# Instance norm on one core: 4 MB units in 32 KB rows against 8 MB units in 64 KB rows, with 4 MB units at both ends

## The chip, the cores and the metric

One core of one Trainium2 chip. The metric is the device time of one execution of the kernel in microseconds, the median of several runs. The core has engines with queues of their own: TensorE (PE) for matmuls, VectorE (DVE), ScalarE (ACT), GpSimd (POOL) and SyncE (SP), which here only issues transfers. Sixteen DMA engines move data between the chip's memory (HBM) and the core's own memory (SBUF, 128 partitions). SP, ACT and POOL each have a DMA queue.

## The reference

For each of 4 x 128 channels (four batches of 8 groups of 16 channels) of 256 x 256 numbers in float32, the mean and the variance over the 65,536 numbers are taken, and the channel is normalised and multiplied by its gamma:

```python
mu = x.mean(axis=(3, 4), keepdims=True)
var = ((x - mu) ** 2).mean(axis=(3, 4), keepdims=True)
x_norm = (x - mu) / np.sqrt(var + 1e-5)
out = x_norm * gamma[None, :, :, None, None]
```

The input is 134.2 MB and so is the output. Each number is read once and written once.

## The kernel before

The 512 channels are taken in 32 units of 16 channels. A channel lies over 8 partitions, so that a unit is a tile of 128 partitions x 8,192 numbers: a row of 32 KB in each partition, 4 MB in all, which is one contiguous stretch of HBM. Six slots of this size (`xt`, line 45) hold the units in SBUF; unit u uses slot u modulo 6.

The order of work on each engine is the order in which the program is written (manual schedule). First come two small transfers on POOL's queue: zeros into a small part of the output (`touch`, line 54, 16 rows of 512 B; the unit's own store writes over them later) and gamma (line 55, 16 rows of 32 B). Then the loads of units 0 to 5 are issued, 1 and 3 on ACT's queue and the others on SP's (lines 56 and 57). VectorE has 60 empty instructions. The averaging matrix `navg` (lines 66 to 76, -1/65,536 within the 8 x 8 blocks of one channel) is made on POOL; gamma is spread over the partitions by a copy on VectorE and eight small matmuls (lines 83 to 94) into `g_col`.

Then for each unit, in the loop from line 105:

- VectorE sums each row (line 107) while ScalarE sums its squares (line 108) into `st`.
- TensorE multiplies `st` by `navg` (line 116), which gives each partition its channel's -mean and -mean of squares (`ps`).
- VectorE makes minus the variance from it (line 117), ScalarE the root (line 121), VectorE the reciprocal (line 125), and the product with gamma (line 127).
- VectorE normalises the tile in place (line 130): (x - mean) * scale.
- ACT issues the store (line 134), and SP the load of unit u + 6 (line 136, line 48), which waits until the store of unit u has landed, for they share the slot.

So in steady work SP's queue holds loads and ACT's queue holds stores, and each of the sixteen DMA engines takes packets from both.

Of the kernel before, what the change touches and what calls it, by code (L numbers as in the profile page):

```python
# [1 line left out]

# [4 lines left out]

F32 = mybir.dt.float32
U8 = mybir.dt.uint8
ALU = mybir.AluOpType  # L10
ACTF = mybir.ActivationFunctionType
AX = mybir.AxisListType


@with_exitstack
def kernel(
    ctx: ExitStack,
    tc: tile.TileContext,
    x: bass.AP,
    gamma: bass.AP,  # L20
    out: bass.AP,
):
    nc = tc.nc
    B, G, C, H, W = x.shape
    P = nc.NUM_PARTITIONS
    HW = H * W
    n_ch = B * G * C
    S = 8
    K = P // S
    F = HW // S  # L30
    U = n_ch // K
    NG = (G * C) // K
    AHEAD = 6
    assert HW % S == 0 and (G * C) % K == 0

    xv = x.rearrange("b g c h w -> (b g c h w)").rearrange("(u p f) -> u p f", p=P, f=F)
    ov = out.rearrange("b g c h w -> (b g c h w)").rearrange("(u p f) -> u p f", p=P, f=F)
    gv = gamma.rearrange("g c -> (g c)")

    data = ctx.enter_context(tc.tile_pool(name="data", bufs=1))  # L40
    singles = ctx.enter_context(tc.tile_pool(name="singles", bufs=1))
    psum = ctx.enter_context(tc.tile_pool(name="psum", bufs=4, space=bass.MemoryType.PSUM))
    ctx.enter_context(tc.manual_schedule())

    slots = [data.tile([P, F], F32, name=f"xt{i}") for i in range(AHEAD)]

    def load(u, queue):
        queue.dma_start(out=slots[u % AHEAD][:], in_=xv[u])  # L48


    g_row = singles.tile([1, G * C], F32, name="g_row")
    touch = singles.tile([16, 128], F32, name="touch")
    nc.vector.memset(touch[:], 0.0)  # L53
    nc.gpsimd.dma_start(out=ov[0][0::S, 0:128], in_=touch[:])  # L54
    nc.gpsimd.dma_start(out=g_row[:], in_=gv[None, :])  # L55
    for u in range(AHEAD):
        load(u, nc.scalar if u in (1, 3) else nc.sync)

    for _ in range(60):
        nc.vector.nop()  # L60

    eps_t = singles.tile([P, 1], F32, name="eps_t")
    nc.gpsimd.memset(eps_t[:], 1e-5)
    one = singles.tile([1, 1], F32, name="one")
    nc.gpsimd.memset(one[:], 1.0)
    navg = singles.tile([P, K, S], F32, name="navg")
    nc.gpsimd.memset(navg[:], -1.0 / HW)  # L67
    nc.gpsimd.affine_select(  # L68
        out=navg[:], in_=navg[:], pattern=[[-S, K], [0, S]], compare_op=ALU.is_ge,
        fill=0.0, base=0, channel_multiplier=1,  # L70
    )
    nc.gpsimd.affine_select(  # L72
        out=navg[:], in_=navg[:], pattern=[[S, K], [0, S]], compare_op=ALU.is_ge,
        fill=0.0, base=S - 1, channel_multiplier=-1,
    )
    navg_w = navg[:].rearrange("p k s -> p (k s)")
    root_eps = singles.tile([P, 1], F32, name="root_eps")
    nc.scalar.activation(out=root_eps[:], in_=eps_t[:], func=ACTF.Sqrt)  # L78
    g_rep = singles.tile([1, NG, K, S], F32, name="g_rep")
    g_ps = psum.tile([P, NG], F32, name="g_ps", bufs=1)  # L80
    g_col = singles.tile([P, NG], F32, name="g_col")

    nc.vector.tensor_copy(  # L83
        out=g_rep[:],
        in_=g_row[:].rearrange("o (n k) -> o n k", n=NG).unsqueeze(3).to_broadcast([1, NG, K, S]),
    )
    for n in range(NG):
        nc.tensor.matmul(  # L88
            out=g_ps[:, n : n + 1],
            lhsT=g_rep[:, n].rearrange("o k s -> o (k s)"),  # L90
            rhs=one[:],
            start=True, stop=True,
        )
    nc.vector.tensor_copy(out=g_col[:], in_=g_ps[:])  # L94

    junk = singles.tile([P, F], U8, name="junk")

    st = singles.tile([P, U, 2], F32, name="st")
    nvar = singles.tile([P, U], F32, name="nvar")
    std = singles.tile([P, U], F32, name="std")  # L100
    rstd = singles.tile([P, U], F32, name="rstd")
    scale = singles.tile([P, U], F32, name="scale")

    squares = []
    for u in range(U):
        t = slots[u % AHEAD]
        nc.vector.reduce_sum(out=st[:, u, 0:1], in_=t[:], axis=AX.X)  # L107
        square = nc.scalar.activation(  # L108
            out=junk[:], in_=t[:], func=ACTF.Square, accum_out=st[:, u, 1:2],
        )  # L110
        if u:

            tc.declare_no_dep(square.ins, squares[-1].ins, reason="junk, ordered by the root between")
        squares.append(square)
        ps = psum.tile([P, 2], F32, name="ps")
        nc.tensor.matmul(out=ps[:], lhsT=navg_w, rhs=st[:, u], start=True, stop=True)  # L116
        nc.vector.tensor_scalar(  # L117
            out=nvar[:, u : u + 1], in0=ps[:, 0:1], scalar1=ps[:, 0:1],
            scalar2=ps[:, 1:2], op0=ALU.mult, op1=ALU.add,
        )  # L120
        nc.scalar.activation(  # L121
            out=std[:, u : u + 1], in_=nvar[:, u : u + 1], func=ACTF.Sqrt,
            bias=eps_t[:], scale=-1.0,
        )
        nc.vector.reciprocal(out=rstd[:, u : u + 1], in_=std[:, u : u + 1])  # L125
        g = u % NG
        nc.vector.tensor_mul(  # L127
            out=scale[:, u : u + 1], in0=rstd[:, u : u + 1], in1=g_col[:, g : g + 1],
        )
        nc.vector.tensor_scalar(  # L130
            out=t[:], in0=t[:], scalar1=ps[:, 0:1], scalar2=scale[:, u : u + 1],
            op0=ALU.add, op1=ALU.mult,
        )
        nc.scalar.dma_start(out=ov[u], in_=t[:])
        if u + AHEAD < U:
            load(u + AHEAD, nc.sync)


# [1 line left out]
_INS = ['x', 'gamma']  # L140
_OUTS = [((4, 8, 16, 256, 256), 'float32')]


# [23 lines left out]
```

## Time and profile before

| what | value |
|---|---|
| time, median of 3 runs (lowest to highest) | 626.78 us (626.75 to 626.82) |
| span of the profiled execution | 625.8 us |
| DMA traffic | 268.46 MB in 9,282 packets, 429 GB/s over the span |
| VectorE busy | 443.4 us (71%) |
| ScalarE busy | 238.8 us (38%) |
| TensorE busy | 21.4 us (3%) |
| row sums (line 107), one | 8,684 ns |
| row sums of squares (line 108), one | 7,030 ns |
| normalising (line 130), one | 4,550 ns |
| median time from issue to landing, loads on SP's queue | 38.5 us |
| the same, stores on ACT's queue | 62.5 us |

The span is the time from the first to the last instruction of one execution that was profiled; the runs are timed without a profile, and include 1.0 us more. An engine's busy share is an average over the whole span. The time from issue to landing of a transfer includes its wait behind earlier transfers of its queue.

### The profile page before, as it was taken

The numbers are of one execution on the slowest core, as the hardware profiler recorded it, in microseconds if no ns is written. First come the engines' busy times: TensorE is split into PE (matmuls) and PEld (weight loads), VectorE is DVE, ScalarE is ACT, GpSimd is POOL, SyncE is SP. The second block draws the span as 40 slices with busy tenths as digits, with TensorE's granted clock in tenths as the row PEclk, the third lists the DMA queues.
The fourth block names the chain that finished last, engine by engine and source line by source line (L and its number), as shares of the span: only waits on it lengthen the run. The fifth ranks groups of instructions, "written<-read, shape, count | busy, mean of one in ns | idle before, by whom it ended". The sixth has DMA issues, their size and how long they took to land.

```text
span 625.8 us, 631 instructions
## 1 busy us (share of the span) xinstructions
PE 21.4 (3%) x80; PEld 19.5 (3%) x80; DVE 443.4 (71%) x163; ACT 238.8 (38%) x98; POOL 2.4 (0%) x11
## 2 busy tenths in 40 slices
PE   0200000000000000000000000000000000000000
PEld 0200000000000000000000000000000000000000
DVE  0588999999776687766776667867668676686730
ACT  0444444444443244432344423444224442244400
POOL 1000000000000000000000000000000000000000
DMA  8999999999999999999999999999999999999998
GB/s 369 436 415 429 429 436 436 436 436 434 424 434 434 434 436 434 431 429 434 436 436 436 436 431 427 431 436 431 436 434 434 429 434 436 436 436 436 429 425 354
DMA packets 9282, 268.46 MB, mean 429 GB/s; under 512 B 1072, under 2 KB 1088, under 8 KB 1088
## 3 DMA queue, kind: packets, MB, share of 16 engines
q10 hardware_dynamic: 4896, 142.61, 52.9%
q1 hardware_dynamic: 4320, 125.83, 46.7%
q0 software_dynamic: 64, 0.01, 0.0%
q14 instruction: 2, 0.02, 0.0%
HBM read 134.22 MB, written 134.23 MB: 429 GB/s over the span
## 4 chain that ended last, share of the span: by engine, by line
another core or an unknown queue 61%; DMA 17%; DVE 15%; SPq 1%; PE 1%; issue 0%; ACT 0%
DVE st L107 10%; DMA xt<-in_x_dram 10%; DMA out_dram<-xt 8%; DVE xt L130 5%; SPq L48 1%; PE ps L116 1%; ACT std L121 0%; DVE nvar L117 0%; DVE rstd L125 0%; DVE scale L127 0%
## 5 line engine op out<-in xcount | busy, mean ns | idle before, releaser
L107 DVE TENSOR_REDUCE st<-xt 128x1 f32<-128x8192 f32 x32 | 277.9, 8684 | 101.2 <-DMA xt<-in_x_dram 101.2
L108 ACT ACTIVATE junk<-xt 128x8192 uint8<-128x8192 f32 x32 | 225.0, 7030 | 276.0 <-DMA xt<-in_x_dram 232.8
L130 DVE TENSOR_SCALAR xt<-xt,ps,scale 128x8192 f32<-128x8192 f32 x32 | 145.6, 4550 | 1.2
L121 ACT ACTIVATE std<-nvar,eps_t 128x1 f32<-128x1 f32 x32 | 9.4, 294 | 79.6 <-DVE nvar L117 79.6
L116 PE MATMUL ps<-st,navg 128*128 128x2 f32 x64 | 17.9, 349 | 558.0 <-DVE st L107 558.0
L116 PEld LDWEIGHTS ps<-st,navg 128*128 128x128 f32 x64 | 16.0, 311 | 559.8 <-issue 559.8
L117 DVE TENSOR_SCALAR nvar<-ps 128x1 f32<-128x1 f32 x32 | 9.2, 287 | 23.8 <-PE ps L116 23.8
L125 DVE RECIPROCAL rstd<-std 128x1 f32<-128x1 f32 x32 | 5.2, 164 | 11.6 <-ACT std L121 11.6
L83 DVE COPY g_rep<-g_row 1x1024 f32<-1x1024 f32 x1 | 0.7, 680 | 14.3 <-DMA g_row<-in_gamma_dram 14.3
L108 ACT ACTIVATION_READ_ACCUMULATOR junk<-xt 128x1 f32 x32 | 6.0, 187 | 0.0
L127 DVE TENSOR_TENSOR scale<-rstd,g_col 128x1 f32<-128x1 f32 x32 | 5.1, 159 | 1.1
L88 PE MATMUL g_ps<-one,g_rep 1*128 1x1 f32 x16 | 3.5, 346 | 16.2 <-DVE g_rep L83 16.2
L88 PEld LDWEIGHTS g_ps<-one,g_rep 1*128 1x128 f32 x16 | 3.5, 325 | 16.1 <-issue 16.1
L94 DVE COPY g_col<-g_ps 128x8 f32<-128x8 f32 x1 | 0.2, 166 | 3.7 <-PE g_ps L88 3.7
L78 ACT ACT_TABLE_LOAD x1 | 1.3, 1283 | 1.7 <-PEq L151 1.7
L53 DVE MEMSET touch<- 16x128 f32 x1 | 0.2, 165 | 0.9 <-PEq L151 0.9
L54 POOL DMA_DIRECT2D out_dram<-touch x1 | 0.6, 619 | 0.8 <-DVE touch L53 0.8
L55 POOL DMA_DIRECT2D g_row<-in_gamma_dram x1 | 0.5, 487 | 0.0
L68 POOL TENSOR_SCALAR_AFFINE_SELECT navg<-navg 128x128 f32<-128x128 f32 x1 | 0.4, 400 | 0.1
L72 POOL TENSOR_SCALAR_AFFINE_SELECT navg<-navg 128x128 f32<-128x128 f32 x1 | 0.4, 399 | 0.1
L67 POOL MEMSET navg<- 128x128 f32 x1 | 0.2, 232 | 0.0
L78 ACT ACTIVATE root_eps<-eps_t 128x1 f32<-128x1 f32 x1 | 0.2, 202 | 0.0
(6 smaller groups left out, 0.6 us busy)
## 6 DMA issues: line engine op xcount, KB each, us to landing
out_dram<-xt ACTq DMA_DIRECT2D x32, 4096.0 KB, 62.5
xt<-in_x_dram SPq DMA_DIRECT2D x30, 4096.0 KB, 38.5
xt<-in_x_dram ACTq DMA_DIRECT2D x2, 4096.0 KB, 31.6
out_dram<-touch POOLq DMA_DIRECT2D x1, 8.0 KB, 9.1
g_row<-in_gamma_dram POOLq DMA_DIRECT2D x1, 0.5 KB, 13.3
```

The lines of the kernel that those rows point to most:

```text
L48: queue.dma_start(out=slots[u % AHEAD][:], in_=xv[u])
L78: nc.scalar.activation(out=root_eps[:], in_=eps_t[:], func=ACTF.Sqrt)
L83: nc.vector.tensor_copy(out=g_rep[:], in_=g_row[:].rearrange("o (n k) -> o n k", n=NG).unsqueeze(3).to_broadcast([1, NG, K, S]),)
L88: nc.tensor.matmul(out=g_ps[:, n : n + 1], lhsT=g_rep[:, n].rearrange("o k s -> o (k s)"), rhs=one[:], start=True, stop=True,)
L107: nc.vector.reduce_sum(out=st[:, u, 0:1], in_=t[:], axis=AX.X)
L108: square = nc.scalar.activation(out=junk[:], in_=t[:], func=ACTF.Square, accum_out=st[:, u, 1:2],)
L116: nc.tensor.matmul(out=ps[:], lhsT=navg_w, rhs=st[:, u], start=True, stop=True)
L117: nc.vector.tensor_scalar(out=nvar[:, u : u + 1], in0=ps[:, 0:1], scalar1=ps[:, 0:1], scalar2=ps[:, 1:2], op0=ALU.mult, op1=ALU.add,)
L121: nc.scalar.activation(out=std[:, u : u + 1], in_=nvar[:, u : u + 1], func=ACTF.Sqrt, bias=eps_t[:], scale=-1.0,)
L125: nc.vector.reciprocal(out=rstd[:, u : u + 1], in_=std[:, u : u + 1])
L127: nc.vector.tensor_mul(out=scale[:, u : u + 1], in0=rstd[:, u : u + 1], in1=g_col[:, g : g + 1],)
L130: nc.vector.tensor_scalar(out=t[:], in0=t[:], scalar1=ps[:, 0:1], scalar2=scale[:, u : u + 1], op0=ALU.add, op1=ALU.mult,)
```

## The change

- A big unit has 32 channels over 4 partitions each: 128 rows of 64 KB, 8 MB. There are 14 of them, in three slots of 64 KB per partition, which take the same space as the six of before.
- Before and after them stand two small units each, of 16 channels as before; a pair shares one slot, half of each row for each. So there are 18 units, numbered 0 to 17: 0, 1, 16 and 17 are small.
- All loads are issued on SP's queue. At the start those of units 0 to 3 are issued. Unit 4 is loaded when units 0 and 1 have been stored; then unit u + 3 when unit u has been stored; units 16 and 17 both after the store of unit 13.
- The squares of a big unit are summed in two halves on ScalarE, into two columns of `st`. The matmul has three columns for it, and one more small instruction of VectorE (`rest`) joins the second half to the root, as its bias.
- There are two averaging matrices, for 8 and for 4 partitions per channel. Gamma is loaded as 32 rows of 4 single numbers, after the four loads have been issued, and is spread by three matmuls with 0/1 matrices. `touch`, the 60 empty instructions and the spreading copy are gone.

The core of the diff:

```diff
-    slots = [data.tile([P, F], F32, name=f"xt{i}") for i in range(AHEAD)]
+    slots = [data.tile([P, FB], F32, name=f"xt{i}") for i in range(SLOTS)]
...
+    def small(pair):
+        nonlocal first, turn
+        for h in range(2):
+            units.append((first, 8, slots[turn % SLOTS][:, h * FS : (h + 1) * FS]))
+            first += KS
+        turn += 1
...
+    small(0)
+    while first < n_ch - KB:
+        units.append((first, 4, slots[turn % SLOTS][:]))
+        first += KB
+        turn += 1
+    small(1)
...
-    nc.gpsimd.dma_start(out=ov[0][0::S, 0:128], in_=touch[:])
-    nc.gpsimd.dma_start(out=g_row[:], in_=gv[None, :])
-    for u in range(AHEAD):
-        load(u, nc.scalar if u in (1, 3) else nc.sync)
...
-    for _ in range(60):
-        nc.vector.nop()
...
+    def load(u):
+        nc.sync.dma_start(out=units[u][2], in_=rows(flat_x, u))
...
+    for u in range(4):
+        load(u)
+    with nc.allow_non_contiguous_dma(reason="128 numbers"):
+        nc.gpsimd.dma_start(out=g_kn[:], in_=gamma.rearrange("g c -> (g c)").rearrange("(n k) -> k n", k=KB))
...
+    for i in range(3):
+        nc.tensor.matmul(out=g_ps[:, i], lhsT=pick[i], rhs=g_kn[:], start=True, stop=True)
     nc.vector.tensor_copy(out=g_col[:], in_=g_ps[:])
...
+        c0, s, t = units[u]
+        parts = 8 // s
+        nc.vector.reduce_sum(out=st[:, u, 0:1], in_=t, axis=AX.X)
+        for h in range(parts):
+            square = nc.scalar.activation(
+                out=junk[:], in_=t[:, h * FS : (h + 1) * FS], func=ACTF.Square,
+                accum_out=st[:, u, 1 + h : 2 + h],
+            )
...
+        if parts == 2:
+            bias = rest[:, u : u + 1]
+            nc.vector.tensor_scalar(
+                out=bias, in0=ps[:, 2:3], scalar1=-1.0, scalar2=1e-5, op0=ALU.mult, op1=ALU.add,
+            )
...
-        nc.scalar.dma_start(out=ov[u], in_=t[:])
-        if u + AHEAD < U:
-            load(u + AHEAD, nc.sync)
+        nc.scalar.dma_start(out=rows(flat_o, u), in_=t)
+        if u == 1:
+            load(4)
+        elif 2 <= u and u + 3 < U - 1:
+            load(u + 3)
+            if u + 3 == U - 2:
+                load(U - 1)
```

## The prediction

> **What bounds the kernel now.** I read the page's row of DMA shares first, then the traffic by queue in a steady stretch, then the queue that SyncE waits with, and last the end of the timeline. The page, its 40 slices (busy tenths of VectorE, of the 16 DMA engines, and GB/s):
>
> ```profile
> DVE  0588999999776687766776667867668676686730
> DMA  8999999999999999999999999999999999999998
> GB/s 369 436 415 429 429 436 436 436 436 434 424 434 434 434 436 434 431 429 434 436 436 436 436 431 427 431 436 431 436 434 434 429 434 436 436 436 436 429 425 354
> ```
>
> The DMA engines are full from the second slice to the last but one, whatever VectorE does (it is at 6 to 7 tenths in the second half). The same by stretches (length, busy engines, then clock, DMA share, GB/s at the end of each line):
>
> ```profile
> 0.00:2.00 2.00, 0.00 (x0) 0.00 (x0) 0.17 (x1) 0.28 (x1) 0.84 (x6) 1.00 0.42 115
> 200.00:500.00 300.00, 8.92 (x32) 8.01 (x32) 216.19 (x80) 117.65 (x48) 0.00 (x0) 1.00 1.00 433
> 586.00:601.00 15.00, 0.56 (x2) 0.50 (x2) 13.71 (x5) 7.42 (x3) 0.00 (x0) 1.00 1.00 430
> 601.00:615.00 14.00, 0.00 (x0) 0.00 (x0) 0.14 (x1) 0.00 (x0) 0.00 (x0) 1.00 1.00 433
> 623.00:626.00 3.00, 0.00 (x0) 0.00 (x0) 0.00 (x0) 0.00 (x0) 0.00 (x0) 1.00 0.03 11
> ```
>
> 433 GB/s in the middle, and the same 430 to 433 at the end, where only stores are left. So direction and mixture cost nothing; only the start (2 us) and the last 2.7 us are not full. In the steady stretch the two queues have equal shares, and each load takes 38.5 us to land, twice its 19.36 us period:
>
> ```profile
> q10 hardware_dynamic: 2224, 65.01, 50.2%
> q1 hardware_dynamic: 2218, 64.82, 50.0%
> ...
> xt<-in_x_dram SPq DMA_DIRECT2D x15, 4096.0 KB, 38.5
> ```
>
> That is because load u+6 is issued when store u has landed, while the load before it is still running:
>
> ```profile
> SPq L48 <- DMA out_dram<-xt: 535.3, 26, 59.6
> ```
>
> And the end: the last load lands at 586.12, its unit is computed in 15.05 us, and its store is issued at 601.17. DMA does not notice, since three stores are queued at 586 (7 equal 4 MB transfers of 9.68 us make up the last 67 us):
>
> ```profile
> 586.12 8.69 DVE L107 TENSOR_REDUCE st<-xt 128x1 f32<-128x8192 f32 x1 [4.33 <-DMA xt<-in_x_dram]
> ...
> 596.59 4.55 DVE L130 TENSOR_SCALAR xt<-xt,ps,scale 128x8192 f32<-128x8192 f32 x1
> 601.17 0.34 ACTq L134 DMA_DIRECT2D out_dram<-xt  x1
> ```
>
> So the time is the bytes at full rate plus idle DMA, and a change can only move the cost of a byte or leave DMA idle. The profiled execution spans 625.8 us, 1.0 below the median of 626.78; I add differences to 626.8.
>
> **How a DMA engine shares.** The trace's packet records: every row of a tile is one packet, 32,768 B in 1,213 ns, and each DMA ends with a 4 B completion packet on each engine. At 7.2 us the GpSimd queue joins the two load queues: on each engine its 512 B row, its completion, the 32 B gamma row and its completion start 2.43 us apart (7.23, 9.67, 12.09, 14.52), which is twice 1,213 ns. So each queue with work gets **one packet a turn, however long it is**. While all rows have 32 KB, that is an equal split. With 64 KB rows beside 32 KB rows it is 2 to 1.
>
> **The change, part by part.**
> 1. *Cost of a byte.* A 512 B packet took 27 ns, a 32 KB one 1,213: 1,186 ns for 32,256 B, 0.03677 ns a byte, and 8 ns fixed. Eight rows of 32 KB are 9.639 us by bytes alone; a DMA takes 19.36/2 = 9.68. So some 0.04 us a DMA are not bytes. 64 DMAs become 36, each still with 8 rows per engine: 28 x 0.042 = **-1.2 us**. No 64 KB row is in this trace. Bounds: 0 (the row is cut into two packets), and -2.7 (64 x 0.042, all of it gone). I take -1.2, the nearest row's law.
>  The Trainium skill (DMA: Bandwidth & Descriptors, Anatomy of one DMA) gives about 2.0 us fixed plus bytes/436 GB/s for one DMA, by which 28 fewer would be worth 56 us. The trace disagrees: 9.68 us from one store's landing to the next, where that law has 11.6. The fixed part lies under the next DMA's data.
> 2. *Start.* All first loads go on SP. Unit 0 is in after about 1.8 + 9.7 + 0.9 = 12.4 us instead of 22.6, but VectorE has g_col's copy ahead of it, which needs gamma. Gamma is now 128 numbers of 4 B, 8 packets and a completion per engine instead of the four turns above; with one load queue a turn is 1.21 us, so 9 x 1.21 = 10.9 from about 7 us, then three of the matmul pairs (3.5/8 = 0.44 each) and the copy: about 20 us, as 19.9 before. DMA has 24 MB of loads (58 us) in hand. Following rows one by one: stores 0 and 1 land at about 64 and 80.5, loads 2 and 3 at 46 and 75, and unit 2 is computed at about 78, so store 2 is there just before store 1 ends. 0, but without slack: each us by which unit 0 starts after 20 leaves up to one us of DMA idle near 80. Bounds 0 and +2. The dropped touch, nops and copies (0.7 us at most each) are beside loads: 0.
> 3. *Middle.* A unit costs VectorE 2 x 8.69 + 1.77 (reduce end to normalise start) + 0.29 (one more L117-like row) + 2 x 4.55 = 28.5 us of a 38.6 us period; the squares, 2 x 7.2, lie beside the reduce. Per slot: load 38.6, compute 28.5, store 38.6, some 3 of landing and issue: 109 against three periods, 116. There is always a store queued; 0. If that fails, stores run alone at the same 433 GB/s, and still nothing is lost.
> 4. *Tail.* Let T be the end of load 15 and store 13. Loads 16 and 17 (32 KB rows) run beside stores 14 and 15 (64 KB rows): a turn of both is 1.21 + 2.41 = 3.62 us. Load 16: 8 turns, T+29.0. Store 15 is there at T + 0.3 (landing) + 28.5 + 0.1 + 1.0 (issue to first packet, 0.81 to 1.80 at the start) = 29.9, so load 17 has one row alone, then 7 turns: T + 55.6. Then 0.3 + 15.05 + 1.0: store 17's first packet at T+72. All other bytes left at T are 7 x 4 MB, done at T + 7 x 9.66 = 67.6. DMA is idle **+4.5 us**, which before's tail was not. Without the row alone it would be 6.9; with an equal split by bytes, 0.
> 5. More waits: SP's load 17 stands right behind load 16, both on store 13; nothing else is queued behind. ACT's next squares stand behind the store's issue, as before. 0.
>
> Sum: 626.8 - 1.2 + 4.5 = **630.1** (profiled span about 629).
>
> **Why T is one point, and the rivals.** After a store lands (0.33 us after its last packet) the next load's packets come 1.0 to 1.6 us later (0.81 to between 1.80 and 2.43 over the engines at the start): 1.35 to 1.95 us, less than one 64 KB row (2.41). So the next store gets one row ahead, then both alternate, and the store's completion waits its turn behind the load's last row: both end in the same round, and this repeats.
> - *Stores lead by a row more* (no loss). If the engines are spread (a store's 16 completions come 0.4 us apart before 150 us, 1.6 after), the wait passes 2.41 us on some and their stores gain a second row. Then at T store 14 has 7 rows left: load 16 takes 7 x 3.62 + 1.21 = 26.6, load 17 is alone until 29.9 (2.7 rows), the other 5.3 turns end at T+49; store 17 starts at T+65.5, DMA has work until 67.6 - 2.4 = 65.2. Idle 0.3: 626.8 - 0.9 = 625.9. It decides from a wait of 2.41 us on. For it: the spread of 1.6; against it: 0.4 in the undisturbed stretch. Chance 0.23, for 625.6 to 628 (partly led).
> - *Late start on top of the tail*: gamma's 4 B packets later than I count. +1 to +3: 631 to 634. Chance 0.15.
> - *Cheaper rows and a covered tail*: -2.7 (part 1's lower end) and 0 to 1 idle, 624.1 to 625.4. Chance 0.12.
> - *The rows are cut in two* (the change does less than it says): two 32 KB packets a row, an even split by bytes, no idle, no gain: 626.5 to 626.8. Its chance is in the first rival's 0.23.
> - *64 KB rows run slower*: the row pitch doubles in HBM; each per cent of a packet's time costs 6.2 us (619.5 us of full DMA), 2 per cent 639. The 1,213 ns show no such loss at 32 KB. Chance 0.05. The Trainium skill (DMA: Bandwidth & Descriptors, Latency and other measured facts) has a rate falling from 214 to 207 GB/s at a 512 KiB row pitch; no run here shows it.
> - The forecast itself, 628 to 632: 0.45.
>
> **How the numbers follow.** About 0.2% (1.25 us) is what a measurement of this kernel can tell from no change. Slower: 0.45 + 0.15 + 0.05 = 0.65. Same: 0.23. Faster: 0.12. The range, 624.5 to 634.0, leaves out the slow rows (0.05) and what of the cheaper rows and of the late start lies farthest out (some 0.1); it takes in parts 1, 2 and 4 up to their ends (0 + 2 + 4.5, or 6.9 alone; -2.3 below).
>
> **What would show it.** In the changed kernel's trace: packets of 65,536 B of about 2,418 ns (1); unit 0's reduce near 20 us, not 12 (2); no DMA slice below 9 tenths between 100 and 600 us (3); load 16 landing about 29 us after load 15 and load 17 26 to 29 us later, and a hole of some 4.5 us in the DMA about 17 us before the end (4). No hole and the loads evenly 19 us apart would make part 4 wrong; a hole near 80 us would make part 2 wrong.

## The result, and the profile after

The changed kernel takes 629.3 us (median of 6 runs, 628.92 to 630.82) beside 626.85 us before (6 runs, 626.75 to 627.51): a ratio of 1.0041, with a 95% interval of 1.003 to 1.0053; the medians lie 2.45 us apart. The forecast was 630.1. Here and below a run that is over 1.5% above the fastest of its kernel counts as slow: it is left out of the ratios (one run each of e5 and e9, two of e12), but not out of the medians. Its profiled execution spans 627.8 us and was timed at 629.47, close to the median; the span of before in the prediction, 625.8, is at the slow end of its own runs (624.9 to 625.9 where it was measured beside the experiments), so that the two profiles differ by 2.0 us and the medians by 2.45.

The page after, the same rows as were shown of before:

```profile
DVE  1978897097692956929569395792948839499780
DMA  9999999999999999999999999999999999999997
GB/s 363 438 401 451 411 457 418 451 418 451 418 447 422 447 422 447 414 451 418 451 418 451 413 455 413 455 405 464 401 468 401 468 401 468 401 447 420 449 411 303
```

DMA is still full. But for the first and the last two slices GB/s swings between 401 and 468 from slice to slice: that is counting, since a packet is counted in the slice where it starts and 64 KB rows are coarse beside 15.7 us slices. By stretches (length, busy engines, clock, DMA share, GB/s):

```profile
400.00:500.00 100.00, 1.68 (x6) 1.50 (x6) 74.51 (x18) 39.44 (x15) 0.00 (x0) 1.00 1.01 438
597.00:612.00 15.00, 0.56 (x2) 0.50 (x2) 13.21 (x5) 7.42 (x3) 0.00 (x0) 1.00 0.95 411
612.00:614.00 2.00, 0.00 (x0) 0.00 (x0) 0.64 (x1) 0.00 (x0) 0.00 (x0) 1.00 0.80 344
620.00:623.00 3.00, 0.00 (x0) 0.00 (x0) 0.00 (x0) 0.00 (x0) 0.00 (x0) 1.00 0.86 371
623.00:628.00 5.00, 0.00 (x0) 0.00 (x0) 0.00 (x0) 0.00 (x0) 0.00 (x0) 1.00 0.17 72
```

The middle is as full as before. The hole that was forecast at the end is there, but shallow: 0.95 and then 0.80 at 597 to 614 us, while the last unit is finished. (A share over two microseconds is coarse, since packets are counted where they start; the packet records below give 0.45 us of idle time for it.) At 620 to 623 us the share is no lower than that of before in the same stretch:

```profile
620.00:623.00 3.00, 0.00 (x0) 0.00 (x0) 0.00 (x0) 0.00 (x0) 0.00 (x0) 1.00 0.83 360
```

But after 623 us 17% of five microseconds is still moved, where before moved 3% of three: the last packet ends later, and the DMA engines do not finish together. The tail's computation, from the timeline:

```profile
578.77 0.34 ACTq L163 DMA_DIRECT2D out_dram<-xt  x1
...
593.70 0.34 ACTq L163 DMA_DIRECT2D out_dram<-xt  x1
597.62 8.69 DVE L128 TENSOR_REDUCE st<-xt 128x1 f32<-128x8192 f32 x1 [3.96 <-DMA xt<-in_x_dram]
...
612.67 0.34 ACTq L163 DMA_DIRECT2D out_dram<-xt  x1
```

These are the stores of units 15, 16 and 17. VectorE waited 3.96 us for load 17, which landed 46.8 us after load 15 (550.84), where two loads at the even pace of before, 19.4 us each, would take 38.8.

**Where the 2 us went.** I added up the packet records of the two traces, as a mean over the 16 engines. Packets at their usual lengths (1,213 ns for 32 KB, **2,418 ns for 64 KB**) come to 621.06 us before and 619.26 after: 1.8 saved. Time by which packets ran longer than that: 1.65 before, 3.04 after, 1.4 lost (0.5 of it in the first 60 us, where before has 1.38 and after 1.89; 0.9 later). Idle engines, from the start to the last packet of any: 3.27 before, 4.92 after, 1.65 lost; of it 0.35 lies near 6 us (six engines wait 0.6 to 1.2 us), 0.45 near 613 us, and the rest, some 0.9, at the end. These three give +1.25 of the +1.78 by which the last packet ends later (626.27 against 624.49); the other 0.5 is the balance of two small items: records of one engine overlap by a few ns, which fewer packets do less (0.8 lost), and there are fewer completions (0.3 saved). The 16 completions of the last store lie 1.6 us apart before and 3.0 after.

### The profile page after: what moved, and what is told of

Read it like the earlier page. It is cut to its first block, busy times and chain, and to the rows that moved or that the text cites. A ratio compares the mean times of both kernels' runs of the same rounds, so it can differ in the third digit from the quotient of the medians.

```text
span 627.8 us, 434 instructions
## 1 busy us (share of the span) xinstructions
PE 11.4 (2%) x42; PEld 10.4 (2%) x42; DVE 429.4 (68%) x105; ACT 234.7 (37%) x84; POOL 6.2 (1%) x21
## 4 chain that ended last, share of the span: by engine, by line
DMA 63%; DVE 26%; another core or an unknown queue 7%; PE 1%; issue 0%; ACT 0%; SPq 0%
DMA xt<-in_x_dram 36%; DMA out_dram<-xt 28%; DVE st L128 16%; DVE xt L159 8%; PE ps L138 1%; ACT std L151 0%; DVE nvar L141 0%; SPq L70 0%; DVE rstd L155 0%; DVE scale L156 0%; DVE rest L148 0%
## 5 line engine op out<-in xcount | busy, mean ns | idle before, releaser
L128 DVE TENSOR_REDUCE st<-xt 128x1 f32<-128x16384 f32 (+1 forms) x18 | 275.8, 15323 | 151.5 <-DMA xt<-in_x_dram 151.5
L159 DVE TENSOR_SCALAR xt<-xt,ps,scale 128x16384 f32<-128x16384 f32 (+1 forms) x18 | 141.7, 7870 | 0.7
L151 ACT ACTIVATE std<-nvar,rest 128x1 f32<-128x1 f32 x14 | 4.1, 294 | 57.0 <-DVE rest L148 57.0
L138 PE MATMUL ps<-st,navg 128*128 128x3 f32 (+1 forms) x36 | 10.0, 349 | 586.4 <-DVE st L128 586.4
L138 PEld LDWEIGHTS ps<-st,navg 128*128 128x128 f32 x36 | 9.0, 311 | 587.4 <-issue 587.4
L141 DVE TENSOR_SCALAR nvar<-ps 128x1 f32<-128x1 f32 x18 | 5.2, 287 | 13.4 <-PE ps L138 13.4
L155 DVE RECIPROCAL rstd<-std 128x1 f32<-128x1 f32 x18 | 3.0, 164 | 6.5 <-ACT std L151 6.5
L151 ACT ACTIVATE std<-nvar,eps_t 128x1 f32<-128x1 f32 x4 | 1.2, 294 | 9.5 <-DVE nvar L141 9.5
L156 DVE TENSOR_TENSOR scale<-rstd,g_col 128x1 f32<-128x1 f32 x18 | 2.9, 159 | 0.6
L148 DVE TENSOR_SCALAR rest<-ps 128x1 f32<-128x1 f32 x14 | 2.1, 148 | 0.0
```

The costliest lines, as they stand in the source:

```text
L128: nc.vector.reduce_sum(out=st[:, u, 0:1], in_=t, axis=AX.X)
L138: nc.tensor.matmul(out=ps[:, : 1 + parts], lhsT=navg[s], rhs=st[:, u, : 1 + parts], start=True, stop=True,)
L141: nc.vector.tensor_scalar(out=nvar[:, u : u + 1], in0=ps[:, 0:1], scalar1=ps[:, 0:1], scalar2=ps[:, 1:2], op0=ALU.mult, op1=ALU.add,)
L148: nc.vector.tensor_scalar(out=bias, in0=ps[:, 2:3], scalar1=-1.0, scalar2=1e-5, op0=ALU.mult, op1=ALU.add,)
L151: nc.scalar.activation(out=std[:, u : u + 1], in_=nvar[:, u : u + 1], func=ACTF.Sqrt, bias=bias, scale=-1.0,)
L156: nc.vector.tensor_mul(out=scale[:, u : u + 1], in0=rstd[:, u : u + 1], in1=gamma_of(u),)
```

## The experiments

Each experiment has one trace, so figures of its DMA engines are of one execution. The theory after reading the two traces was that the loss lies in the tail: 32 KB loads beside 64 KB stores. The rivals were the 64 KB rows themselves, all over the run, and the new start. The median of the kernel before, measured beside each on the same chip, stands in its row.

| run | what it changes in the changed kernel | us (runs) | before, beside it | last store's completions, us apart |
|---|---|---|---|---|
| changed kernel | | 629.30 (6) | 626.85 | 3.0 |
| e1 | stores of units 14 and 15 in 32 KB half rows | 629.13 (5) | 626.88 | 4.1 |
| e2 | all rows 32 KB | 627.84 (11) | 626.88 | 1.0 |
| e3 | gamma on ACT's queue | 632.03 (6) | 626.88 | 0.6, after a hole; 6.6 the store before |
| e4 | no small pair at the end | 642.14 (2) | 626.88 | 0.2, after a hole |
| e5 | e1 and e3 | 630.66 (7) | 627.14 | 4.7 |
| e6 | e2, loads issued later | 628.10 (12) | 627.14 | 1.0 |
| e7 | 64 KB rows, 64 partitions a transfer | 734.74 (4) | 627.14 | |
| e8 | the kernel before, with the new start | 627.65 (11) | 627.14 | 1.6 |
| e9 | only loads in 32 KB half rows | 658.79 (6) | 626.87 | |
| e10 | only stores in 32 KB half rows | 627.64 (11) | 626.87 | 1.2 |
| e11 | the old start | 635.28 (6) | 626.87 | 0.6, after a hole; 5.8 the store before |
| e12 | e2 and the old start | 628.29 (12) | 626.87 | 5.6 |

**e1: the tail's stores in half rows.**

```diff
-        nc.scalar.dma_start(out=rows(flat_o, u), in_=t)
+        if u in (U - 4, U - 3):
+            for h in range(2):
+                nc.scalar.dma_start(
+                    out=rows(flat_o, u)[:, h * FS : (h + 1) * FS], in_=t[:, h * FS : (h + 1) * FS],
+                )
+        else: ...
```

> The changed kernel, but the stores of the last two big units (14 and 15) go as two transfers of 32 KB half rows, so that they share the DMA engines evenly with the loads of units 16 and 17. Theory (the loss is the 2 to 1 turn in the tail, which lets load 17 land 8.8 us later on the engines that are behind, 0.45 us of mean DMA idleness near 612 us and a wider finish): load 17 lands with a spread under 3 us instead of 8.8, no hole at 612 us, about 628.0 us. Rival (64 KB rows cost by themselves, by longer packets all over the run): unchanged at 629.3.

Load 17 landed with a spread of 3.1 us over the engines instead of 8.8, and the hole near 612 us is gone: by the packet records no engine is idle from 600 to 618 us.

```profile
597.00:612.00 15.00, 0.56 (x2) 0.50 (x2) 10.28 (x5) 4.36 (x3) 0.00 (x0) 1.00 1.03 443
612.00:614.00 2.00, 0.00 (x0) 0.00 (x0) 0.00 (x0) 0.00 (x0) 0.00 (x0) 1.00 0.88 377
```

The loss of time stayed: 629.13 (ratio 1.0034, 1.0022 to 1.0046). In this trace the engines were 4.1 us apart in each load from 354 to 513 us, and they finished 4.1 us apart. My theory had taken the tail's hole for the loss; the lag was older than the tail. Up to the store of unit 14 e1 is the same program as the changed kernel, whose engines were 2.6 to 3.1 us apart in that stretch: the lag differs by a microsecond from one execution to another.

**e2: no 64 KB row anywhere.** Each transfer of a big unit is two, and a half load waits for the store of its half only.

```diff
-        nc.sync.dma_start(out=units[u][2], in_=rows(flat_x, u))
+        for h in range(8 // units[u][1]):
+            nc.sync.dma_start(
+                out=units[u][2][:, h * FS : (h + 1) * FS], in_=rows(flat_x, u)[:, h * FS : (h + 1) * FS],
+            )
...
-        nc.scalar.dma_start(out=rows(flat_o, u), in_=t)
+        for h in range(parts):
+            nc.scalar.dma_start(
+                out=rows(flat_o, u)[:, h * FS : (h + 1) * FS], in_=t[:, h * FS : (h + 1) * FS],
+            )
```

> The changed kernel with every big load and store cut into two transfers of 32 KB half rows: same units, slots, order and computation, but no 64 KB packet anywhere. Theory (everything lost comes from the long rows, in the tail and in packets that ran over 2418 ns, and 1.0 us is gained by them): the gain of 1.0 is given back, 1.3 of the tail and up to 1.4 of long packets return, 626.9 to 628. Rival (three slots or the new start cost the time, whatever the rows): 629.3 plus the 1.0 us of fixed packet cost, 630.3.

627.84 us (1.0015, 1.0006 to 1.0023), 1.5 less than the changed kernel though the fixed cost of 28 transfers is back. After 60 us there are all but no long packets (0.1 us in the mean), the engines stay 1.0 us apart to the end, and there is no hole:

```profile
597.00:612.00 15.00, 0.00 (x0) 0.00 (x0) 4.49 (x1) 0.00 (x0) 0.00 (x0) 1.00 1.02 439
620.00:623.00 3.00, 0.00 (x0) 0.00 (x0) 0.00 (x0) 0.00 (x0) 0.00 (x0) 1.00 1.06 459
623.00:626.00 3.00, 0.00 (x0) 0.00 (x0) 0.00 (x0) 0.00 (x0) 0.00 (x0) 1.00 0.04 14
```

So in this kernel the long rows cost more than they save.

**e3 and e5: gamma on ACT's queue.**

```diff
-        nc.gpsimd.dma_start(out=g_kn[:], ...
+        nc.scalar.dma_start(out=g_kn[:], ...
```

> The changed kernel with gamma loaded from ScalarE's queue instead of GpSimd's. In the changed kernel's trace six DMA engines stand idle for 0.6 to 1.2 us near 6.3 us, just before the first packet of GpSimd's queue, and these six are the ones that are late in the tail. Theory (GpSimd's queue causes that hole, and the head start it gives the others is what opens the tail): no hole at 6 us, load 17 lands with a spread under 4 us, about 628.3 us. Rival (the hole comes from the single load queue at the start, or the spread from later long packets): hole and spread stay, 629.3.

> Gamma on ScalarE's queue (as in e3) and the stores of units 14 and 15 in 32 KB half rows (as in e1). e3's trace has a hole of 5.0 us at 613 to 618 us, after load 17 landed 18.6 us later on the last engine than on the first. Theory (the uneven turns in the tail make that hole, from engines that are 7 us apart before it): load 17's spread no wider than before it, no hole, 632.0 - 5.0 = 627 to 629 us. Rival (e3's time comes from gamma's place, not from the tail): 631 to 632.

The hole near 6 us went, the first loads land 0.5 us apart instead of 1.0, and yet e3 takes 632.03 (1.0103, 1.0066 to 1.0139; its runs lie between 631 and 640): the engines drift 7.3 us apart by 506 us all the same, and then the tail has a hole of the size of part 4 of the prediction. Load 17 landed 18.6 us later on the last engine than on the first, and 50.0 us after load 15 on the last engine of each, not 55.6; so the sizes agree, but not the count of rows. The stretches of e3:

```profile
602.00:613.00 11.00, 0.56 (x2) 0.50 (x2) 9.15 (x4) 7.42 (x3) 0.00 (x0) 1.00 0.90 387
613.00:618.00 5.00, 0.00 (x0) 0.00 (x0) 4.70 (x2) 0.00 (x0) 0.00 (x0) 1.00 0.11 46
618.00:628.00 10.00, 0.00 (x0) 0.00 (x0) 0.00 (x0) 0.00 (x0) 0.00 (x0) 1.00 0.98 423
```

For five microseconds VectorE alone works (4.70 of 5.00) and DMA moves a tenth. e5 evens the turns in the tail: no such hole, 630.66 (1.0065, 1.004 to 1.0091), but with its own drift of 4.7 us, and runs from 628.9 up to 643.7. So the tail's uneven turns are real and make a hole of five microseconds where the engines come to it 7 us apart. The drift is another thing: it is there with gamma on either queue.

**e4: the tail's price, exposed.** The loop of big units goes on to the last channel.

```diff
-    while first < n_ch - KB:
+    while first < n_ch:
...
-    small(1)
...
```

> The changed kernel without the small pair at the end: units 0 and 1 small, then 15 big ones to the end. Theory (the price of the tail is compute of the last unit plus issue minus the stores still queued): the last load ends with 6 rows of the store before it left, 14.5 us; 0.3 + 28.4 us of work and 1.0 to the first packet make 29.7; idle 15.2, about 642 us. Rival (the end is hidden or depends on something else): under 635.

642.14 us (1.0241, 1.0224 to 1.0259), as worked out. The last store but one ends at 603.4 to 607.6 us, and the last comes at 619.9:

```profile
603.00:605.00 2.00, 0.00 (x0) 0.00 (x0) 2.00 (x1) 2.00 (x1) 0.00 (x0) 1.00 0.08 33
605.00:619.00 14.00, 0.56 (x2) 0.50 (x2) 12.82 (x6) 0.69 (x3) 0.00 (x0) 1.00 0.01 5
619.00:639.00 20.00, 0.00 (x0) 0.00 (x0) 0.01 (x1) 0.00 (x0) 0.00 (x0) 1.00 0.97 419
```

(Packets count where they start, so the share falls one row early.) The rule, work of the last unit less the stores still queued, holds to a microsecond here: the engines are idle for 15.5 us in the mean between 600 and 620 us, and 15.2 were worked out.

**e6 and e7: is it the load queue that runs nearly dry?** In e6 the two half loads of a unit are issued in the other order, so that both wait for the whole slot; in e7 a transfer takes the even or the odd partitions, with rows left at 64 KB.

e6 beside e2:

```diff
-        for h in range(8 // units[u][1]):
+        for h in reversed(range(8 // units[u][1])):
```

e7 beside the changed kernel (n and parts are 2 for a big unit; stores likewise):

```diff
-        nc.sync.dma_start(out=units[u][2], in_=rows(flat_x, u))
+        for h in range(n):
+            nc.sync.dma_start(out=units[u][2][h::n], in_=rows(flat_x, u)[h::n])
```

> e2 (32 KB half rows everywhere), but the two loads of a unit are issued in the other order, so that both wait for the second store of the slot. In e2 the first half load goes out 19 us before the slot is wholly free, so that load queue always has 12 us in hand; in the changed kernel it has only 5. Theory (what pulls the engines apart is a load queue that runs nearly dry, so that a load's first row shows its latency on some engines): the spread of the 16 engines grows past 2 us and the time goes to 628.5 or more. Rival (it is the length of the row alone): spread 1.0 to the end and 627.8, as e2.

> The changed kernel with 64 KB rows as they are, but each big load and store as two transfers of 64 rows, the even and the odd partitions, so that the load of one half goes out when the store of that half has landed, some 19 us earlier. Theory (dry load queue): first rows of loads no longer over 2418 ns, spread at the end under 2 us, about 627 us or below. Rival (row length alone): spread and time as the changed kernel, 629.3. If 64 partitions at a step of two feed the engines unevenly it is slower than both, which a lower GB/s in the middle would show.

e6: 628.10 (1.0019, 1.001 to 1.0029). No first row of a load is long after 60 us and the last stores' completions are 1.0 us apart, but those of the loads drift to 2.2 us, where e2's stay at 1.0. So a late issue may pull the loads apart a little; it costs no time that these runs can tell from e2's, and the theory falls as the cause of the loss, at least for 32 KB rows. e7 says nothing on it: transfers over every other partition ran at 347 GB/s in the middle (734.74 us), for a reason that no run here shows.

```profile
200.00:500.00 300.00, 3.35 (x12) 3.01 (x12) 160.28 (x36) 87.28 (x30) 0.00 (x0) 1.00 0.95 347
```

**e9 and e10: loads or stores?** One side in half rows as in e2 (e9 has the loads' part of its diff, e10 the stores'), the other at 64 KB.

> The changed kernel with the big loads cut into 32 KB half rows, the stores left at 64 KB. In every trace with 64 KB rows the packets that run long after 60 us are nearly all loads' (2536 to 3349 ns instead of 2418), and the kernels without 64 KB rows (e2, e6) have none and finish with the engines 1.0 us apart. Theory (long load rows pull the engines apart): few long packets, spread at the end near 1 us, half of the fixed cost saved: 627.3 to 628. Rival (two long rows side by side, or long stores): long packets stay, 629 or more.

> The changed kernel with the big stores cut into 32 KB half rows, the loads left at 64 KB. Theory (long load rows pull the engines apart): long load packets stay, the engines finish 3 us or more apart, about 629; the tail shares evenly, so no hole near 612 us. Rival (long stores, or the pair of both): 627.3 to 628.

I had the sides the wrong way round. e10, long loads beside short stores, takes 627.64 (1.0013, 1.0004 to 1.0021): undoing the **stores'** long rows alone brings 1.7 us back. The load rows in it still have 64 KB, but after 60 us its packets run over their usual length by 0.5 us in the mean, not by 1.15 as in the changed kernel, and the end is clean:

```profile
620.00:623.00 3.00, 0.00 (x0) 0.00 (x0) 0.00 (x0) 0.00 (x0) 0.00 (x0) 1.00 1.04 448
623.00:626.00 3.00, 0.00 (x0) 0.00 (x0) 0.00 (x0) 0.00 (x0) 0.00 (x0) 1.00 0.00 0
```

e9, short loads beside long stores, takes 658.79 (1.0516, 1.0479 to 1.0553). That is the tail's mixture in the whole run. By the turns of part 4, a load row beside a store row takes 3.62 us and one alone 1.21, so that an engine that moved fewer load rows alone is 2.4 us later for each of them; and one load does land up to 29 us later on the last engine than on the first. Then all slots come to VectorE together and DMA stands:

```profile
358.00:367.00 9.00, 0.00 (x0) 0.00 (x0) 9.00 (x2) 0.38 (x1) 0.00 (x0) 1.00 0.06 25
```

Idle DMA engines are 14 of the 26 us by which the last packet of e9's trace ends later than that of before; the other 12 are packets that ran over their usual length, more than half of it on 64 KB store rows.

**e8, e11 and e12: the start.** e8 is the kernel before with all first loads on SP and without touch and empty instructions (gamma is loaded as before, and six loads are issued first, not four); e11 gives the changed kernel touch and unit 1's load on ACT's queue back; e12 adds that to e2.

```diff
...
+    nc.gpsimd.dma_start(out=rows(flat_o, 0)[0::8, 0:128], in_=touch[:])
     for u in range(4):
-        load(u)
+        load(u, nc.scalar if u == 1 else nc.sync)
...
```

> The kernel before with the changed kernel's start alone: no touch, no empty instructions, all first loads on SP's queue. The prediction's step 2: nothing, 626.9, since DMA is full either way, with unit 0 starting when gamma is there. Rival (the changed kernel loses time at its start, through the hole near 6.3 us): 627.2 to 628.

> The changed kernel with parts of the start of before: the touch of the output ahead of gamma on GpSimd's queue, and the load of unit 1 on ScalarE's queue. e8 (the new start in the kernel before) was 0.1 per cent slower, and e2 (no long rows) still 0.15 per cent. Theory (the start costs 0.5 to 0.9 us whatever the rows): 628.4 to 628.8. Rival (the start's price is that of e8 alone, or is made up for later by the slots): 629.3.

> Both parts undone: 32 KB half rows everywhere (e2) and the start of e11; what is left of the change are the big units, the three slots and the small pairs. Theory (long rows and start are all of it): as the kernel before, 626.9 to 627.3. Rival (three slots or the last part of the program cost time as well): stays at e2's 627.8.

e8: 627.65 (1.0009, 1.0001 to 1.0018), some 0.5 us for the start, just clear of noise; its trace shows more long packets at 28 to 150 us (1.45 us against 0.8 before). In the changed kernel the old start is no cure but the worst start of those tried: 635.28 (1.0123, 1.0103 to 1.0143), with first rows of loads that run 0.5 us long (75 of them), load 17 spread over 15 us and a hole of 3.4 us at 616 to 624. With 32 KB rows (e12) it is unclear: 628.29 in the median (1.003, 1.0011 to 1.0049), six of twelve runs at 627.1 to 627.5 and the others between 629 and 646. The trace is of one of the others, 631.60 us, and it matters: no row in it has 64 KB, and yet the completions of its loads drift from 3.0 us apart at 274 us to 6.8 at 549, its last store's are 5.6 apart, and packets run over by 0.7 us after 60 us.

```profile
200.00:500.00 300.00, 4.47 (x16) 4.01 (x16) 210.56 (x48) 107.03 (x39) 0.00 (x0) 1.00 1.00 432
623.00:629.00 6.00, 0.00 (x0) 0.00 (x0) 0.00 (x0) 0.00 (x0) 0.00 (x0) 1.00 0.17 71
```

So long rows are not needed for the engines to drift. The first 20 us decide over 629 or 635 with long rows, and over a steady or a scattered time with 32 KB rows. That they do it by the way in which the turns fall is my reading; no run shows it, and which order is good was not found by a rule.

No kernel beat the one before.

## Why the prediction was right, and where its steps were not

The time (629.3 for 630.1) and the sign were right, but both by luck. The term that carried the forecast, 4.5 us of idle DMA in the tail, came out at 0.45; with that the sum gives 626.8 - 1.2 + 0.45 = 626.05, a little faster than before. In its place came some 2.6 us that were not in the sum: 1.4 of packets over their usual length, 0.9 of engines that finish apart and 0.35 near 6 us.

1. *Cost of a byte: right.* A 64 KB row is one packet, 2,418 ns, exactly the law of the nearest rows (8 ns + 0.03677 ns a byte). The records save 1.8 us at usual lengths and 0.3 of completions, and lose 0.8 of overlap: 1.2 to 1.3 net, and 1.2 were taken. The Trainium skill's law that part 1 cites (DMA: Bandwidth & Descriptors, Anatomy of one DMA) is given there for transfers issued from GpSimd. The 9.68 us are of transfers on ACT's queue, so that the trace does not test the law; it shows only that here no such 2 us stand between queued transfers. What was not taken into the sum: packets over their usual length, +1.4 us, or 0.2%, unevenly over the engines. A rival at 0.05 ("64 KB rows run slower") had this cost, but for every row, and the usual 64 KB row is not slower.
2. *Start: the size was off.* Gamma came as one packet of 32 B and a completion per engine, not as eight, and landed 7.6 us after its issue; unit 0 started at 13.90, when load 0 was there, and not near 20. There was no hole near 80 us. A hole near 6 us, 0.35 in the mean, was not foreseen.
3. *Middle: right.* The DMA share is 1.00 or 1.01 in each hundred microseconds from 200 to 500.
4. *Tail: the turns right, the point T wrong.* The records show the turns one for one, a 32 KB load row, a 64 KB store row. But T was not one point: the stores led by two rows (store 13's last packets end at 542.5 to 545.6 us, load 15's at 547.4 to 550.5), as in the first rival, which had a chance of 0.23. Load 16's last packet came 26.6 us after load 15's, the rival's 26.6 and not 29.0; load 17's came 47 us after it, nearer to the rival's 49 than to 55.6; and the hole was 0.45 us in the mean, nearer to the rival's 0.3 than to 4.5. So the rival had the tail right and the forecast had not; the rival's time, 625.9, lacked the same 2.6 us. In e3, where the engines were further apart, the hole was 5.0.
5. *The missing step:* the time is that of the last of 16 engines, not of their mean. I counted the engines as one. e1 shows that the tail can be mended without gain, e2 and e10 that the lag and most of the loss go when the stores have short rows. e12 shows that this is not the whole cause, since its engines drift without any long row.

By the experiments, long store rows cost 1.7 us net beside long load rows (e10 against the changed kernel) and 31 us beside short ones (e9 against e2). Against before, 0.8 us more remain in e10 and 1.0 in e2. To give 0.5 of this to the start, by e8, is an argument and not shown: what e8's trace shows, 1.45 us of long packets at 28 to 150 us beside 0.8 of before, is not in e2 (0.63) and hardly in e10 (0.95). Two other items are in the traces and were not tested alone: the hole near 6 us, 0.2 to 0.35 us in e2, e6 and e10 and none in before and e8; and the time from the last packet to the end of the span, 1.7 us in these three and 1.3 in before and e8. **Open:** what makes the engines drift, and why long store rows do it with this start where long load rows do not. Of the 33 load rows over 2,500 ns after 60 us in the changed kernel's trace, 15 are the first row of a load; the records do not show what holds them.

The Trainium skill (DMA: Bandwidth & Descriptors, Queues, rings and completion order) says that an engine goes round its queues packet by packet, with typically 9 to 17 descriptors in a packet. The turns agree; here each row took a turn by itself, so that the length of the rows set the shares while both queues had work.

## What to carry to other kernels

Where two queues kept the DMA engines full, each took one row a turn, so the queue with the longer rows got the larger share: give the side that feeds the computation the longer rows (e10) or equal ones (e2), and not long stores beside short loads (e9: 5% slower). The time here was that of the last of 16 engines (after 618 us they stood idle for 2.0 us in the mean, 1.1 before): read how far the completions of one transfer lie apart over the run, not only the mean share. Where transfers are queued anyway, fewer and larger ones save only what shows between them, here 0.04 us each.

## What was not expected of the hardware

- After 60 us, 33 of the 64 KB load rows of the changed kernel take 2,512 to 3,349 ns in place of 2,418, 15 of them the first row of a load. With 32 KB rows on both sides packets run over by only 0.1 us in the mean after 60 us in e2 and e6, but by 0.7 in e12.
- The 16 DMA engines drifted apart over a run, by 3.1 us between the completions of one load in the changed kernel and 7.3 in e3, but also by 6.8 in e12, which has no long row.
- When a store joined late in the tail (issued at 578.77), load rows kept their turns to 582.4 us, 3.6 us after the issue, while the last store, issued with the engine idle, began after 0.8 us.
- A transfer over 64 partitions at a step of two ran the DMA at 347 GB/s in place of 433 (e7).
- A small edit at the start cost 0.5 us in one kernel (e8), and nearly its reverse cost 6 us in another (e11).
